# Ten gate and up chunks of the last FFN in pairs, by seven block products over both halves of the tokens

## The chip, the cores and the metric

One core of a Trainium2 chip. The metric is the device time of one execution in microseconds, as a median of runs. The engines are named as in the profile: PE (TensorE, matmuls), PEld (its weight loads), DVE (VectorE), ACT (ScalarE), POOL (GpSimd), SP (the engine that issues the DMAs).

## The reference

A trunk of two layers over 1024 tokens of 1024 channels, all in float32. Layer 0 mixes the tokens by two attention forms, layer 1 by a convolution module, and each layer ends with an FFN. What follows is what the change touches:

```python
def conformer_conv(h, ...):                 # layer 1
    a = h @ w_pw1 + b_pw1
    u = a[..., :D_MODEL] * jax.nn.sigmoid(a[..., D_MODEL:])
    u = lax.conv_general_dilated(u, w_dw, ...) + b_dw        # causal, 31 taps, each channel by itself
    u = (u - mu) * lax.rsqrt(var + EPS) * ln_g + ln_b        # over the channels
    return jax.nn.silu(u) @ w_pw2 + b_pw2

def swiglu(h, wg, wu, wd):                  # each layer; D_FF = 2816
    return (jax.nn.silu(h @ wg) * (h @ wu)) @ wd

for layer in range(2):
    h = h + mix(rms_norm(h, mix_norm[layer]))
    h = h + swiglu(rms_norm(h, ffn_norm[layer]), ffn_w_gate[layer], ffn_w_up[layer], ffn_w_down[layer])
```

## The kernel before

**Number format.** Every float32 operand is split into a high part and a low part, both of the type fp32r: ACT casts the high part, DVE subtracts it from the source (`split`, L95 to L101). A product is then three matmuls, high by high, high by low, low by high (`mm3`, L205 to L209).

**Tiling.** The tokens are worked on in two halves of 512, which is the moving side of a matmul: all matmuls here are of 128x512. The residual `xres` stands in SBUF as 8 tiles of 128 tokens. An FFN (`ffn_steps`) goes through its 2816 hidden channels in 22 chunks of 128; a chunk is a gate product and an up product, each of 8 K tiles by 3 matmuls, so 48 matmuls. Four chunks are collected, then two `down` steps, one for each half of the 1024 output columns, add act^T w into the residual, which DVE does from PSUM (L230). The weights of a chunk are loaded 256 columns at a time (1 MB) and split beside the matmuls.

**Layer 1.** The work is a list of steps that `run` traces in order; the weights of a step are traced one step ahead. In the names, f10 is the FFN of layer 1 for half 0 of the tokens and f11 that for half 1, p1 the first pointwise product of the convolution module for half 1, pw2 the second. A convolution (`conv_steps`) is 31 multiply-adds of DVE per 128 channels, 248 for a half, on `cv` tiles; `interleave` spreads them in pieces evenly behind the matmul steps given to it, and a piece may not begin before the DVE work of the step ahead of the last one. LayerNorm (`layer_norm`) transposes the `cv` tiles on PE into two PSUM buffers (tag "n", names plt), takes statistics and an inverse root on DVE (bst, mv, nv, nt, lrs, lnb), normalises on ACT (lx); the swish transposes back (pls), ACT makes ls and its high part sh, DVE the low part sl. LayerNorm of half 1 thus needs all 248 multiply-adds, and pw2 needs the swish.

The order of half 1's convolution module among the FFN of half 0 is this list (f10 has 34 steps: 22 chunks and 12 down steps):

```python
[lambda: add_bias(1), p1[0], norm_step(0, ffng[1], "f10")]
+ interleave(p1[1:] + f10[:21], conv_steps(1))
+ interleave(f10[21:27], ln1) + f10[27:-4] + pw2(1, s1) + [norm_step(1, ffng[1], "f11")]
+ f10[-4:] + [lambda: store(0, 0), lambda: store(0, 1)]
+ f11[:-1] + [lambda: store(1, 0), f11[-1], lambda: store(1, 1)]
```

**What sets the order.** When the program is built, a scheduler reorders the traced instructions and fixes one order for each engine; on the chip each engine runs its own list in that order and waits by semaphores. Tiles come from pools with a fixed number of buffers, so a load or a split also waits for the last reader of the buffer it takes. The pools `raw` (2 buffers of 8 KB a partition) and `ws` (8 of 4 KB) of the weights last for the whole program.

Of the kernel before, what the change touches and what calls it, by code (L numbers as in the profile page):

```python
# [18 lines left out]
P = 128  # L19
# [6 lines left out]
NF = DFF // P  # L26
EPS = 1e-6
# [7 lines left out]
def r32(ap):  # L35
    return ap.bitcast(F32)
# [3 lines left out]
def trunk(ctx, tc, x, mix_norm, ffn_norm, hy_w_in, hy_w_gate2, hy_b_gate, hy_gla_norm,  # L40
# [8 lines left out]
    raw_p = ctx.enter_context(tc.tile_pool(name="raw", bufs=2))  # L49
    ws_p = ctx.enter_context(tc.tile_pool(name="ws", bufs=8))  # L50
    dram = ctx.enter_context(tc.tile_pool(name="dram", bufs=1, space=DRAM))

# [7 lines left out]
    identr = const.tile([P, P], F32R, name="identr")  # L60
    nc.scalar.copy(identr, ident)
    maskr = const.tile([P, P], F32R, name="maskr")
    hones = const.tile([P, P], F32, name="hones")
    nc.vector.memset(hones, 0.0)
    nc.vector.memset(hones[0:64, 0:64], 1.0 / 64.0)
    nc.vector.memset(hones[64:128, 64:128], 1.0 / 64.0)

    # vectors, 128 channels to a row, transposed on chip into columns
# [34 lines left out]
    small = ctx.enter_context(tc.tile_pool(name="small", bufs=2))  # L103

    def inv_sqrt(y, ss, scale, name):
        """y = 1 / sqrt(ss * scale + eps), by Newton's iteration."""
# [12 lines left out]
    def x_tile(name, dt=F32):  # L119
        return hold.tile([P, 1056], dt, name=name, tag="x", bufs=8)  # L120
# [6 lines left out]
    def norm_stats(xt, junk, name):  # L127
        """1 / RMS of four token tiles."""
# [13 lines left out]
    def norm_half(xt, xn, rs, gcol, ps, pstag, name, muls):  # L142
        """Four token tiles scaled (into xn); returns the transposed hi and lo parts [D chunk, 8, 512]."""
# [11 lines left out]
    def load_cols(w, c0, name, n=256):  # L155
        """n columns of a weight with 1024 rows."""
        raw = raw_p.tile([P, NK, n], F32, name=f"raw_{name}", tag="raw")
        nc.sync.dma_start(raw, w[:, c0:c0 + n].rearrange("(k p) c -> p k c", p=P))
        return raw

    def load_rows(w, r0, n, j, name):
        """n chunks of 128 rows of a weight with 1024 columns, half j of the columns."""
# [10 lines left out]
    # A step is a function, or a pair (weights, body) whose weights are traced one such step ahead.  # L173
    def interleave(main, filler):
        """The main steps in order, with the filler steps spread evenly behind them."""
# [29 lines left out]
    def mm3(ps, sh, sl, mh, ml, first, last):  # L205
        """ps += s^T m by the three leading products of the hi and lo parts."""
        nc.tensor.matmul(ps, sh, mh, start=first, stop=False)  # L207
        nc.tensor.matmul(ps, sh, ml, start=False, stop=False)  # L208
        nc.tensor.matmul(ps, sl, mh, start=False, stop=last)  # L209

    def down(w, r0, acts, xt, tiles, ps, tag, j, name):
        """Step of x[tile] += act^T w over n K chunks, half j of the columns."""
# [25 lines left out]
    def ffn_steps(l, h, hT, xt, ps, ft, act, use_silu, group):  # L238
        raws, acts = {}, {}

        def weights(f):
            if f % 2 == 0:
                raws["g"] = load_cols(ffn_w_gate[l], P * f, f"g{l}{f}{h}")
                raws["u"] = load_cols(ffn_w_up[l], P * f, f"u{l}{f}{h}")
            return [parts(raws[t][:, :, P * (f % 2):P * (f % 2) + P], f"{t}{l}_{f}_{h}") for t in ("g", "u")]
# [21 lines left out]
        while f < NF:  # L267
            n = min(group, NF - f)
# [14 lines left out]
    # Activations that need a table stay between its load and the next one.  # L283
# [20 lines left out]
    # =====================================================================  # L304
    # layer 0: hybrid mixer
    # =====================================================================
# [706 lines left out]
```

## Time and profile before

| | us |
|---|---|
| median of 3 runs (lowest to highest) | 2323.39 (2320.95 to 2323.78) |
| span of the profiled execution | 2319.9 |
| PE busy, 10866 matmuls | 2290.3 (99%) |
| DVE busy | 1591.3 (69%) |
| ACT busy | 922.4 (40%) |
| convolution of half 1, first to last multiply-add | 1468.4 to 1782.2 |
| last matmul starts | 2315.93 |

The profile is of one execution; its busy time of an engine is the time in which at least one of its instructions ran. PE runs matmuls one into the other, so the mean duration of a matmul (391 ns) is longer than the distance between two of them. "Idle before" and the arrow behind it say how long an engine waited and what ended the wait.

### The profile page before, as it was taken

The numbers are of one execution on the slowest core, as the hardware profiler recorded it, in microseconds if no ns is written. First come the engines' busy times: TensorE is split into PE (matmuls) and PEld (weight loads), VectorE is DVE, ScalarE is ACT, GpSimd is POOL, SyncE is SP. The second block draws the span as 40 slices with busy tenths as digits, with TensorE's granted clock in tenths as the row PEclk, the third lists the DMA queues.
The fourth block names the chain that finished last, engine by engine and source line by source line (L and its number), as shares of the span: only waits on it lengthen the run. The fifth ranks groups of instructions, "written<-read, shape, count | busy, mean of one in ns | idle before, by whom it ended". The sixth has DMA issues, their size and how long they took to land.

```text
span 2319.9 us, 27940 instructions
## 1 busy us (share of the span) xinstructions
PE 2290.3 (99%) x10866; PEld 1899.1 (82%) x10866; DVE 1591.3 (69%) x2486; ACT 922.4 (40%) x1506; POOL 32.9 (1%) x39
## 2 busy tenths in 40 slices
PE   7999999999999999999999999999999999999999
PEld 6788888788888887788888888888888888888887
DVE  6687764877788656588888856789998545334334
ACT  6465545655565324523222245422222424222221
POOL 0000000000000001000000002000000000000000
PEclk9999999999999999999999999999999999999999
DMA  6254454233343235233222322322322223322322
GB/s 207 97 163 141 167 188 141 76 98 118 100 131 111 68 103 181 73 97 103 91 93 89 109 91 82 109 86 96 109 91 91 91 92 127 109 91 92 108 84 80
DMA packets 206387, 253.74 MB, mean 109 GB/s; under 512 B 8709, under 2 KB 156272, under 8 KB 206254
## 3 DMA queue, kind: packets, MB, share of 16 engines
q1 hardware_dynamic: 206254, 251.95, 33.5%
q8 instruction: 85, 1.39, 0.2%
q14 instruction: 48, 0.39, 0.1%
HBM read 230.95 MB, written 20.97 MB: 109 GB/s over the span
## 4 chain that ended last, share of the span: by engine, by line
PE 95%; DMA 2%; DVE 2%; ACT 1%; issue 0%; SPq 0%; ACTq 0%; DVEq 0%
PE po L207 9%; PE po L209 9%; PE po L208 9%; PE pu L207 7%; PE pu L209 7%; PE pu L208 7%; PE pg L207 7%; PE pg L209 7%; PE pg L208 7%; PE pp L208 2%; PE pp L207 2%; PE pp L209 2%; PE po L652 2%; PE wt L634 1%; PE z L617 1%; PE z L613 1%
## 5 line engine op out<-in xcount | busy, mean ns | idle before, releaser
L908 DVE SCALAR_TENSOR_TENSOR cv<-u,wd,cv 128x512 f32<-128x512 f32 x480 | 358.1, 749 | 9.9
L230 DVE TENSOR_TENSOR xr<-xr,po 128x512 f32<-128x512 f32 x296 | 202.1, 684 | 168.8 <-PE po L209 168.0
L207 PE MATMUL po<-wh_d,a 128*128 128x512 f32 x704 | 277.8, 395 | 1.7 <-DVE xr L230 1.6
L207 PE MATMUL pg<-hh_f,wh_g 128*128 128x512 f32 x704 | 275.8, 392 | 3.6 <-DVE s L260 3.6
L208 PE MATMUL pg<-hl_f,wh_g 128*128 128x512 f32 x704 | 276.6, 393 | 0.0
L209 PE MATMUL pg<-hh_f,wl_g 128*128 128x512 f32 x704 | 275.8, 392 | 0.0
L209 PE MATMUL po<-wh_d,a 128*128 128x512 f32 x704 | 275.5, 391 | 0.0
L208 PE MATMUL pu<-hl_f,wh_u 128*128 128x512 f32 x704 | 275.4, 391 | 0.0
L208 PE MATMUL po<-wl_d,a 128*128 128x512 f32 x704 | 275.2, 391 | 0.0
L209 PE MATMUL pu<-hh_f,wl_u 128*128 128x512 f32 x704 | 275.2, 391 | 0.0
L207 PE MATMUL pu<-hh_f,wh_u 128*128 128x512 f32 x704 | 275.0, 391 | 0.0
L97 ACT CAST wh_g<-raw_g 128x1024 fp32r<-128x1024 f32 x88 | 92.8, 1054 | 348.4 <-PE po L208 226.2
L97 ACT CAST wh_d<-raw_d 128x1024 fp32r<-128x1024 f32 x88 | 92.5, 1053 | 252.0 <-PE pu L208 116.7
L98 DVE TENSOR_TENSOR wl_g<-raw_g,wh_g 128x1024 fp32r<-128x1024 f32 x88 | 107.6, 1223 | 88.0 <-ACT wh_g L97 83.8
L207 PEld LDWEIGHTS po<-wh_d,a 128*128 128x128 f32 x704 | 132.3, 188 | 31.4 <-DVE xr L230 4.0
L207 PEld LDWEIGHTS pg<-hh_f,wh_g 128*128 128x128 f32 x704 | 132.6, 188 | 30.8 <-DVE s L260 3.8
L209 PEld LDWEIGHTS po<-wh_d,a 128*128 128x128 f32 x704 | 132.2, 188 | 27.8
L209 PEld LDWEIGHTS pg<-hh_f,wl_g 128*128 128x128 f32 x704 | 132.7, 189 | 27.0
L208 PEld LDWEIGHTS pu<-hl_f,wh_u 128*128 128x128 f32 x704 | 132.3, 188 | 27.3
L261 DVE TENSOR_TENSOR s<-s,pu 128x512 f32<-128x512 f32 x88 | 60.5, 687 | 137.1 <-PE pu L209 134.5
L208 PEld LDWEIGHTS pg<-hl_f,wh_g 128*128 128x128 f32 x704 | 132.6, 188 | 26.7
L209 PEld LDWEIGHTS pu<-hh_f,wl_u 128*128 128x128 f32 x704 | 132.2, 188 | 27.0
(318 smaller groups left out, 4300.3 us busy)
## 6 DMA issues: line engine op xcount, KB each, us to landing
raw_g<-in_ffn_w_gate_dram SPq DMA_DIRECT2D x44, 1024.0 KB
raw_u<-in_ffn_w_up_dram SPq DMA_DIRECT2D x44, 1024.0 KB
raw_d<-in_ffn_w_down_dram SPq DMA_DIRECT2D x30, 1024.0 KB
raw_p<-in_cv_w_pw_dram SPq DMA_DIRECT2D x16, 1024.0 KB
raw_d<-in_ffn_w_down_dram SPq DMA_DIRECT2D x28, 512.0 KB
raw_wo<-in_hy_w_out_dram SPq DMA_DIRECT2D x8, 1024.0 KB
raw_q<-in_cv_w_pw_dram SPq DMA_DIRECT2D x8, 1024.0 KB
kr<-k_d SPq DMA_DIRECT2D x48, 128.0 KB
```

The costliest lines, as they stand in the source:

```text
L97: nc.scalar.copy(hi, src)
L98: nc.vector.tensor_sub(lo, src, r32(hi))
L207: nc.tensor.matmul(ps, sh, mh, start=first, stop=False)
L208: nc.tensor.matmul(ps, sh, ml, start=False, stop=False)
L209: nc.tensor.matmul(ps, sl, mh, start=False, stop=last)
L230: nc.vector.tensor_add(xt[i][:, cs], xt[i][:, cs], po)
L261: nc.vector.tensor_mul(s, s, pr[1])
L613: nc.tensor.matmul(z, qs[:, sub(i)], kh[:, s0:s0 + w], start=True, stop=False)
L617: nc.tensor.matmul(z, qs[:, sub(i)], kl[:, s0:s0 + w], start=False, stop=True)
L634: nc.tensor.transpose(pt[:, col:col + P], wrow[bi][:, P * j:P * j + P], ident)
L652: nc.tensor.matmul(po[:, lo_c:256], st["v"][j // 4][:, j % 4, e, :], m[:, 256 * jj + lo_c:256 * jj + 256], start=(last and jj == 0 and m i ...
L908: i = nc.vector.scalar_tensor_tensor(acc, u[:, j:j + TH], wd[:, c, j:j + 1], acc, op0=ALU.mult, op1=ALU.add)
```

## The change

The number of FFN chunks that each half does by itself in layer 1 becomes `ALONE` = 12. The other ten are done in five pairs, for both halves of the tokens at once, after everything else. For a pair, the weight matrix is a block matrix of 2x2 (two blocks of 512 rows by two chunks), and so are the tokens (two blocks of 512 channels by two halves). Instead of the eight block products there are seven, of 4 K tiles by 3 matmuls each, on sums and differences of blocks (Strassen's algorithm in Winograd's form). The sums over the token blocks are made once (`sums`, `sum4`, on DVE and ACT, among the chunks of f11); those of the weights for each pair (`pair_weights`). Two of the seven products are evicted half way (to u by ACT, to v by DVE) and continued in the same PSUM tile by another product. The down steps of a pair then run over all eight token tiles.

Since f10 now has 18 steps, the list of half 1's convolution module changes: the convolution stands behind 7 + 10 steps instead of 7 + 21, LayerNorm behind 4 instead of 6, and no chunk stands between LayerNorm and pw2. The weight pools are closed after f10, and the rest runs with new pools that take the same room: smaller and more raw buffers, groups of 2 chunks, loads of 128 columns. All stores of the output are at the end. Constants of layer 0 are moved into its own pool.

```diff
+ALONE = 12
...
-    raw_p = ctx.enter_context(tc.tile_pool(name="raw", bufs=2))
-    ws_p = ctx.enter_context(tc.tile_pool(name="ws", bufs=8))
...
+    weights_es = ctx.enter_context(ExitStack())
+    raw_p = weights_es.enter_context(tc.tile_pool(name="raw", bufs=2))
+    ws_p = weights_es.enter_context(tc.tile_pool(name="ws", bufs=8))
...
-    def ffn_steps(l, h, hT, xt, ps, ft, act, use_silu, group):
+    def ffn_steps(l, h, hT, xt, ps, ft, act, use_silu, group, last=NF, wide=2):
...
-        f10 = ffn_steps(1, 0, lambda: hT["f10"], xres, ps, ft, act, True, 4)
-        f11 = ffn_steps(1, 1, lambda: hT["f11"], xres, ps, ft, act, True, 4)
+        f10 = ffn_steps(1, 0, lambda: hT["f10"], xres, ps, ft, act, True, 4, ALONE)
...
-               norm_step(0, ffng[1], "f10")] + interleave(p1[1:] + f10[:21], conv_steps(1))
-            + interleave(f10[21:27], ln1) + f10[27:-4] + pw2(1, s1) + [norm_step(1, ffng[1], "f11")]
-            + f10[-4:] + [lambda: store(0, 0), lambda: store(0, 1)]
-            + f11[:-1] + [lambda: store(1, 0), f11[-1], lambda: store(1, 1)])
+               norm_step(0, ffng[1], "f10")] + interleave(p1[1:] + f10[:-8], conv_steps(1))
+            + interleave(f10[-8:-4], ln1) + pw2(1, s1) + [norm_step(1, ffng[1], "f11")] + f10[-4:])
+    weights_es.close()
+    with ExitStack() as es:
+        raw_p = es.enter_context(tc.tile_pool(name="raw3", bufs=3))
+        ws_p = es.enter_context(tc.tile_pool(name="ws3", bufs=7))
...
+            BUFS = {"a": 6, "b": 2}
...
+        def product(pm, w, b, first=True, last=True):
+            for k in range(4):
+                mm3(pm, w[:, 0, k, :], w[:, 1, k, :], b[0][:, k, :], b[1][:, k, :], first and k == 0, k == 3,
+                    skip_group_check=not (first and last))
...
+        def pair_products(wt, nm, done):
+            pm = lambda i: ps.tile([P, 512], F32, name=f"ps{i}{nm}", tag="a")
+            p0 = pm(0)
+            product(p0, wt["11"], b11, last=False)
+            u = ft(f"u{nm}")
+            nc.scalar.copy(u, p0)
+            product(p0, wt["12"], b21, first=False)
+            done(0, 0, p0, None)
+            p1 = pm(1)
+            product(p1, wt["s2"], t2)
+            nc.vector.tensor_add(u, u, p1)
+            p2 = pm(2)
+            product(p2, wt["s3"], t3, last=False)
+            p3 = pm(3)
+            product(p3, wt["s1"], t1, last=False)
+            v = ft(f"v{nm}")
+            nc.vector.tensor_add(v, u, p3)
+            done(1, 1, p2, v)
+            product(p3, wt["s4"], b22, first=False)
+            done(0, 1, p3, u)
+            product(p2, wt["22"], t4, first=False)
+            done(1, 0, p2, u)
...
+        f11 = ffn_steps(1, 1, lambda: hT["f11"], xres, ps, s_tile, act, True, 2, ALONE, 1)
+        steps = interleave(f11, [lambda k=k: sums(k) for k in range(4)])
+        steps += [lambda k=k: sum4(k) for k in range(4)]
+        late = []
+        for f in range(ALONE, NF, 2):
+            mats, downs = pair_steps(1, f)
+            steps += mats[:1] + late + mats[1:]
+            late = downs
...
+        run(steps + [late[0], lambda: store(0), late[1], lambda: store(1)])
```

What this does to the built orders is shown at three places. In a row stand the line, the operation, what it writes and what it reads; numbers are part of the names.

PE before, at the last `cv` tile (cv17) of the convolution of half 1. plt10, plt11 are the transposes of the first and second token tile, pg1_16 and pg1_17 gate products of f10:

```order
L207 MATMUL pg1_16_0_14907<-hh_f10_12598,wh_g1_16_0_14757 128x512
L208 MATMUL pg1_16_0_14907<-hl_f10_12599,wh_g1_16_0_14757 128x512
L929 MATMUL plt101_14839<-ident_69,cv17_14589 128x128
L209 MATMUL pg1_16_0_14907<-hh_f10_12598,wl_g1_16_0_14758 128x512
...
L207 MATMUL pg1_17_0_15043<-hh_f10_12598,wh_g1_17_0_14899 128x512
L929 MATMUL plt110_14868<-ident_69,cv10_12723 128x128
...
L929 MATMUL plt110_14868<-ident_69,cv13_13537 128x128
L929 MATMUL plt111_14874<-ident_69,cv14_13769 128x128
...
L929 MATMUL plt111_14874<-ident_69,cv17_14589 128x128
L208 MATMUL pg1_17_0_15043<-hl_f10_12599,wh_g1_17_0_14899 128x512
```

PE after, at the same place, from the last matmul of a down product (po_3_1) on; pls10 are the first transposes of the swish:

```order
L204 MATMUL po_3_1_14472<-wh_d1_4_012_14333,a1_7_0_14011 128x512
L932 MATMUL plt101_14111<-ident_63,cv15_13601 128x128
L932 MATMUL plt101_14111<-ident_63,cv16_13765 128x128
L932 MATMUL plt101_14111<-ident_63,cv17_13929 128x128
L932 MATMUL plt110_14140<-ident_63,cv10_12723 128x128
...
L932 MATMUL plt110_14140<-ident_63,cv13_13209 128x128
L932 MATMUL plt111_14146<-ident_63,cv14_13437 128x128
...
L932 MATMUL plt111_14146<-ident_63,cv17_13929 128x128
L932 MATMUL plt120_14175<-ident_63,cv10_12723 128x128
...
L932 MATMUL plt131_14282<-ident_63,cv17_13929 128x128
L946 MATMUL pls10_14309<-ident_63,lx100_14093 128x128
```

The matmuls of f10 that stood between the transposes are gone from there; the transposes of all four token tiles follow each other.

DVE before, at the end of the convolution; wl are low parts of weights, s and a belong to FFN chunks, bst are the first statistics of LayerNorm:

```order
L908 SCALAR_TENSOR_TENSOR cv17_14589<-u71_13107,wd_8689,cv17_14589 128x512
L98 TENSOR_TENSOR a1_14_0_14735<-s1_14_0_14732,a1_14_0_14735 128x512
L908 SCALAR_TENSOR_TENSOR cv17_14589<-u71_13107,wd_8689,cv17_14589 128x512 x3
L98 TENSOR_TENSOR wl_g1_17_0_14900<-raw_g1160_14753,wh_g1_17_0_14899 128x1024
L908 SCALAR_TENSOR_TENSOR cv17_14589<-u71_13107,wd_8689,cv17_14589 128x512 x2
L261 TENSOR_TENSOR s1_15_0_14815<-s1_15_0_14815,pu1_15_0_14790 128x512
L98 TENSOR_TENSOR wl_u1_17_0_14904<-raw_u1160_14755,wh_u1_17_0_14903 128x1024
L98 TENSOR_TENSOR a1_15_0_14818<-s1_15_0_14815,a1_15_0_14818 128x512
L930 BN_STATS bst10_14829<-plt101_14839 128x6
```

DVE after, from its last add of a down product on (of the 32 convolution rows the first, some of the last and the final six, which are one row):

```order
L225 TENSOR_TENSOR xr3_3194<-xr3_3194,po_3_1_14472 128x512
L90 TENSOR_TENSOR wl_q0112_14520<-raw_q011_14513,wh_q0112_14519 128x1024
L911 SCALAR_TENSOR_TENSOR cv17_13929<-u71_13147,wd_8689,cv17_13929 128x512
L911 SCALAR_TENSOR_TENSOR cv16_13765<-u61_13064,wd_8689,cv16_13765 128x512
L911 SCALAR_TENSOR_TENSOR cv15_13601<-u51_12985,wd_8689,cv15_13601 128x512
...
L911 SCALAR_TENSOR_TENSOR cv17_13929<-u71_13147,wd_8689,cv17_13929 128x512
L911 SCALAR_TENSOR_TENSOR cv16_13765<-u61_13064,wd_8689,cv16_13765 128x512
L911 SCALAR_TENSOR_TENSOR cv17_13929<-u71_13147,wd_8689,cv17_13929 128x512 x6
L933 BN_STATS bst10_14101<-plt101_14111 128x6
L935 BN_AGGR mv10_14102<-bst10_14101 128x2
```

Between the last split and the statistics there are now 32 multiply-adds; before, the last ones stood among the splits and products of f10's chunks 14 to 17.

ACT before, at the first weights of f11; hh_f11 is the high part of the normalised tokens, pt_f11 their transposes, in brackets the semaphores that a row waits for:

```order
L97 CAST wh_d1_20_010_16064<-raw_d1_20_01_16062 128x1024 [waits DMAHW4_49,PE_49]
L100 ACTIVATE hh_f11_15876<-pt_f11_0_15878,vb_86 128x512 [waits PE_49]
L100 ACTIVATE hh_f11_15876<-pt_f11_1_15885,vb_86 128x512 [waits PE_49]
L97 CAST wh_g1_0_1_16104<-raw_g101_16100 128x1024 [waits DMAHW5_49,PE_49]
L100 ACTIVATE hh_f11_15876<-pt_f11_2_15892,vb_86 128x512 [waits PE_49]
L100 ACTIVATE hh_f11_15876<-pt_f11_3_15899,vb_86 128x512 [waits PE_49]
L97 CAST wh_u1_0_1_16108<-raw_u101_16102 128x1024 [waits DMAHW6_49,PE_49]
L100 ACTIVATE hh_f11_15876<-pt_f11_4_15906,vb_86 128x512 [waits PE_49]
```

ACT after, with the casts of the block sums (tt):

```order
L92 ACTIVATE hh_f11_14822<-pt_f11_7_14873,vb_73 128x512 [waits PE_49]
L89 CAST wh_g1_0_1_15171<-raw_g101_15167 128x1024 [waits DMAHW5_49,DVE_49,PE_49]
L89 CAST tt1_15165<-b22_0_15531 128x512 [waits DVE_49,Activation_49]
L89 CAST tt2_15166<-b12_0_15529 128x512
L89 CAST tt0_15164<-b11_0_15527 128x512
L89 CAST wh_u1_0_1_15175<-raw_u101_15169 128x1024 [waits DMAHW6_49]
L89 CAST wh_g1_1_1_15183<-raw_g111_15179 128x1024 [waits DMAHW7_49]
L89 CAST wh_u1_1_1_15187<-raw_u111_15181 128x1024 [waits DMAHW0_49]
L253 ACTIVATE s1_0_1_15241<-pg1_0_1_15191 128x512 [waits DVE_49,PE_49,Activation_49]
```

The cast of the first gate weights, which stood among the evictions of the norm, now stands behind them all, with the casts of the next weights in a row behind it.

## Rows read from the trace of the kernel before

**Rows 1.** The page: the span, then busy time, share and instructions of each engine.

```profile
span 2319.9 us, 27940 instructions
...
PE 2290.3 (99%) x10866; PEld 1899.1 (82%) x10866; DVE 1591.3 (69%) x2486; ACT 922.4 (40%) x1506; POOL 32.9 (1%) x39
```

**Rows 2.** Stretches: length, busy us (x) of PE, PEld, DVE, ACT, POOL; clock, DMA.

```profile
1468.40:1782.20 313.80, 313.80 (x1401) 259.79 (x1400) 285.97 (x376) 85.90 (x103) 1.09 (x5) 1.00 0.29 94
1782.20:1832.80 50.60, 50.60 (x242) 42.17 (x241) 33.18 (x90) 18.07 (x23) 0.00 (x0) 1.00 0.26 85
1960.00:2300.00 340.00, 340.00 (x1502) 281.62 (x1501) 130.28 (x146) 89.31 (x107) 0.00 (x0) 1.00 0.29 97
```

**Rows 3.** Timeline at the end: start us, us, engine, line, operation, count, idle before.

```profile
2315.25 0.39 PE L209 MATMUL po<-wh_d,a 128*128 128x512 f32 x1
...
2315.93 0.39 PE L209 MATMUL po<-wh_d,a 128*128 128x512 f32 x1
2316.36 0.69 DVE L230 TENSOR_TENSOR xr<-xr,po 128x512 f32<-128x512 f32 x1 [0.67 <-PE po L209]
```

**Rows 4.** Groups of DVE, 1468.4 to 1782.2: count, busy us, mean ns, idle before.

```profile
L908 DVE SCALAR_TENSOR_TENSOR cv<-u,wd,cv 128x512 f32<-128x512 f32 x240 | 178.2, 749 | 4.4
L98 DVE TENSOR_TENSOR wl_g<-raw_g,wh_g 128x1024 fp32r<-128x1024 f32 x18 | 22.0, 1223 | 3.7 <-ACT wh_g L97 3.3
...
L230 DVE TENSOR_TENSOR xr<-xr,po 128x512 f32<-128x512 f32 x24 | 16.4, 683 | 2.1 <-PE po L209 1.8
```

**Rows 5.** Timeline of DVE in the convolution of half 1.

```profile
1470.97 1.23 DVE L98 TENSOR_TENSOR wl_p<-raw_p,wh_p 128x1024 fp32r<-128x1024 f32 x1
1472.12 3.11 DVE L908 SCALAR_TENSOR_TENSOR cv<-u,wd,cv 128x512 f32<-128x512 f32 x4
...
1476.03 0.74 DVE L908 SCALAR_TENSOR_TENSOR cv<-u,wd,cv 128x512 f32<-128x512 f32 x1
...
1477.35 0.74 DVE L908 SCALAR_TENSOR_TENSOR cv<-u,wd,cv 128x512 f32<-128x512 f32 x1
```

**Rows 6.** Timeline of one token tile's LayerNorm, half 1: PE, DVE and ACT.

```profile
1809.24 1.04 PE L929 MATMUL plt<-ident,cv 128*128 128x128 f32 x8
...
1810.04 1.29 DVE L930 BATCH_NORM_STATS2 bst<-plt 128x6 f32<-128x512 f32 x2
...
1812.56 0.16 DVE L117 SCALAR_TENSOR_TENSOR lrs<-nt_l,lrs 128x1 f32<-128x1 f32 x1
...
1813.05 0.69 DVE L230 TENSOR_TENSOR xr<-xr,po 128x512 f32<-128x512 f32 x1 [0.33 <-PE po L209]
...
1813.65 0.15 DVE L115 TENSOR_TENSOR nt_l<-lrs 128x1 f32<-128x1 f32 x1
...
1814.81 0.16 DVE L934 SCALAR_TENSOR_TENSOR lnb<-mv,lrs 128x1 f32<-128x1 f32 x1
...
1815.09 1.45 ACT L936 ACTIVATE lx<-plt,lnb,lrs 128x512 f32<-128x512 f32 x2 [6.96 <-DVE lnb L934]
```

**Rows 7.** Timeline: transposes of the swish and the ACT work behind them.

```profile
1837.55 1.03 PE L943 MATMUL pls<-ident,lx 128*128 128x128 f32 x8
1838.19 1.45 ACT L945 ACTIVATE ls<-pls,vb 128x512 f32<-128x512 f32 x2 [0.74 <-PE pls L943]
```

**Rows 8.** Timeline of PE around its longest wait, and a stretch as in rows 2.

```profile
455.94 0.50 PE L207 MATMUL pg<-hh_f,wh_g 128*128 128x512 f32 x1 [3.62 <-DVE s L260]
...
457.43 0.62 PE L207 MATMUL pg<-hh_f,wh_g 128*128 128x512 f32 x1
457.85 0.63 PE L208 MATMUL pg<-hl_f,wh_g 128*128 128x512 f32 x1
...
458.00:459.00 1.00, 1.00 (x4) 0.80 (x3) 0.75 (x2) 0.42 (x1) 0.00 (x0) 0.50 0.06 16
459.00:460.00 1.00, 1.00 (x4) 0.71 (x4) 0.69 (x1) 0.20 (x1) 0.00 (x0) 0.50 0.00 0
```

**Rows 9.** Groups of ACT, 1960 to 2300: count, busy us, mean ns, idle before.

```profile
L97 ACT CAST wh_g<-raw_g 128x1024 fp32r<-128x1024 f32 x20 | 21.0, 1052 | 98.4 <-PE po L208 67.2 <-PE pg L208 28.5 <-DMA raw_g<-in_ffn_w_gate_dram 2.7
```

More of the change, by code (lines that the diff above doesn't have):

```diff
@@ L59, in trunk @@
     nc.vector.memset(one_t, 1.0)
[L60 to L66, printed above, removed]
     rows = lambda ap: ap.rearrange("(k p) -> k p", p=P)
@@ L119, in x_tile @@
     def x_tile(name, dt=F32):
-        return hold.tile([P, 1056], dt, name=name, tag="x", bufs=8)
+        return hold.tile([P, D], dt, name=name, tag="x", bufs=8)
     def h_tile(name):
@@ L203, in run, with mm3 @@
                 s()
[L205 to L209, printed above, removed]
+    def mm3(ps, sh, sl, mh, ml, first, last, **kw):
+        nc.tensor.matmul(ps, sh, mh, start=first, stop=False, **kw)
+        nc.tensor.matmul(ps, sh, ml, start=False, stop=False, **kw)
+        nc.tensor.matmul(ps, sl, mh, start=False, stop=last, **kw)
     def down(w, r0, acts, xt, tiles, ps, tag, j, name):
@@ L235, in sub @@
         return slice(P * (i % 4), P * (i % 4) + P)
-    def ffn_steps(l, h, hT, xt, ps, ft, act, use_silu, group):
+    def ffn_steps(l, h, hT, xt, ps, ft, act, use_silu, group, last=NF, wide=2):
         raws, acts = {}, {}
         def weights(f):
[L242 to L245, printed above, removed]
+            if f % wide == 0:
+                raws["g"] = load_cols(ffn_w_gate[l], P * f, f"g{l}{f}{h}", P * wide)
+                raws["u"] = load_cols(ffn_w_up[l], P * f, f"u{l}{f}{h}", P * wide)
+            c0 = P * (f % wide)
+            return [parts(raws[t][:, :, c0:c0 + P], f"{t}{l}_{f}_{h}") for t in ("g", "u")]
         def chunk(f, ws):
@@ L266, in ffn_steps @@
         steps, late, f = [], [], 0
-        while f < NF:
-            n = min(group, NF - f)
+        while f < last:
+            n = min(group, last - f)
             for c in range(f, f + n):
@@ L362, in trunk @@
         t_tile = lambda name, dt=F32: tp.tile([P, 512], dt, name=name, tag="t")
+        identr = gp.tile([P, P], F32R, name="identr")
+        nc.scalar.copy(identr, ident)
+        maskr = gp.tile([P, P], F32R, name="maskr")
+        hones = gp.tile([P, P], F32, name="hones")
+        nc.vector.memset(hones, 0.0)
+        nc.vector.memset(hones[0:64, 0:64], 1.0 / 64.0)
+        nc.vector.memset(hones[64:128, 64:128], 1.0 / 64.0)
         mtmp = ft("mtmp")
@@ L968, in norm_step @@
             return lambda: hT.update({name: norm(h, gcol, name)})
-        def store(h, j):
-            for i in range(4 * h, 4 * h + 4):
-                cs = slice(512 * j, 512 * j + 512)
-                nc.sync.dma_start(xout[i * P:(i + 1) * P, cs], xres[i][:, cs])
         p0 = pw1_steps(0, lambda: hT["c0"])
```

84 lines of the change are left out of this document (added).

## The prediction

> **What bounds the kernel now.** I read the totals first, then stretches by engine, then single rows. TensorE is busy 99% of a 2319.9 us span, with VectorE at 69% [rows 1]. In the three stretches of layer 1 that the change touches, PE is busy in every microsecond, at full granted clock, while DVE uses 286.0 of 313.8 us, 33.2 of 50.6 and 130.3 of 340 [rows 2]. So until now a matmul taken out of this part is time taken out, and a wait put in is time put in; but in the first stretch DVE has only 9% to spare, and it is the causal convolution that fills it. That is the place to watch.
>
> The profiled execution has a span of 2319.9 us and the median of the runs is 2323.39, 3.5 us above it. I make the sum on the span and add 3.5.
>
> **Matmuls removed.** A 128x512 matmul starts 0.2267 us after the one before: (2315.93 − 2315.25)/3 [rows 3]. The built orders hold 10824 PE instructions before and 10704 after. Ten chunks lose 2 matrices x 2 halves x 24 = 960 matmuls and get 5 pairs x 2 matrices x 7 products x 12 = 840. 120 x 0.2267 = **−27.2 us**, if PE stays fed. No other part of the edit can gain, since PE has no idle time there to give back.
>
> **The convolution loses its cover.** Its DVE instructions for half 1 of the tokens were spread over 28 steps of matmul work and are now spread over 17, because the first half's FFN of layer 1 ends at chunk 12. The built orders give, from the end of the first pointwise chunk to the last transposes of the convolution's result, 1406 matmuls before and 1008 after: about 321 us of PE work against 231 (transposes included). What DVE does between its first and last convolution instruction falls only by 15 weight splits (1.22 us each) and 18 adds or products of 512 columns (0.68 each) [rows 4], 30 us, and by some 10 more since more convolution instructions alternate between two results (below): from 286 to about 245.5. DVE now has more work than PE.
>
> Where this ends is seen in the order. DVE's last add on a down product, xr3 from po_3_1, belongs to the last matmul before the transposes. Behind it DVE has one weight split and 32 convolution instructions, and PE has nothing but transposes that need the last of them. Convolution instructions that alternate with another result start every 0.66 us ((1477.35 − 1476.03)/2); in a chain on one result they start every 0.78 (four in 3.11); a weight split takes 1.15 to the next start (1472.12 − 1470.97) [rows 5]. 27 x 0.666 + 5 x 0.78 = 21.9; with the split (1.15) and the add (0.61) 23.7. PE waits at least about that; the start of the add, 0.43 us behind the start of the last matmul (2316.36 − 2315.93 [rows 3]), and the way back add some 0.8. I take **+24.5 us**. The lower end is 23.6; the upper is DVE idling 9% of the stretch as it did before: 245.6/0.911 − 231.3 = 38.
>
> **LayerNorm loses its cover too.** Before, 139 matmuls stood between the transposes of the first and of the last token tile, and 110 more among the swish; now 0 and 36. The chain of a tile was hidden; now it is the path. The two PSUM buffers of a tile come free only when ACT has normalised it, so the next tile's second transposes wait for that. From the rows of one tile: the second statistics instruction starts about 0.61 behind the first, 1810.65, and the last small DVE step at 1814.81; an unrelated add costs 0.9 of that (from 1812.56 + 0.19 to 1813.65), so 3.26. ACT starts 0.28 later and takes 1.45 for both halves [rows 6]. Four transposes and the hand-off to the next engine are 0.64 (1837.55 to 1838.19) [rows 7]. One tile: 0.64 + 3.26 + 0.28 + 1.45 = 5.6. First tile to its ACT 3.8, three periods 16.9, half a normalisation 0.8: 21.5, of which 25 transposes at 0.1 us are work: **+19 us** (17 to 24).
>
> The swish then starts with little ready: the first pw2 product needs transposes, swish (0.73) and cast, about 2 us, beside 12 transposes that PE can do: **+1.5** (1 to 4).
>
> **The clock.** Before, PE waited 3.62 us once, for DVE; its next matmuls ran at full pace for 1.5 us, and then 8 of them started 0.42 apart instead of 0.23, at a granted clock of 0.50, the lower level of 1.2 GHz, in the stretch 458 to 460 [rows 8]: 8 x 0.2 = 1.6 us, for a single wait. The change has about 45 us of waiting with only transposes in between, in two or three pieces. I take **+3** (1.6 to 10; the upper end is all transposes and the 36 matmuls of the swish at half clock).
>
> The Trainium skill, "TensorE: Matmul & The Clock Gate", section "HAM oscillation — how this bites in real kernels", says that waits which recur between bursts of matmuls let the array fall back to its lower clock each time, so that every burst starts slow. The row above agrees with it for one wait. By the rule at its worst, every burst of the LayerNorm and swish at the lower level, the sum is 7 us higher.
>
> **The new pools.** The first weights of half 1 no longer share pools with the work before: the new pools lie over the old ones, so the cast of the first gate weights waits on ACT for the last matmul of half 0, where it used to stand among the norm's evictions. ACT's cast takes 1.05 [rows 9], then come a few matmuls, then the lower part's split (1.22 [rows 4]). Behind that cast on ACT stand casts for the block sums and the next weights. About 2.1; I take **+2.5** (1.5 to 5, if the next chunk's loads, which wait for the same, come late).
>
> **Inside the seven products.** Two products per matrix are evicted in the middle (to ACT by a copy, to DVE by an add) and then go on in the same PSUM tile. In PE's order at least 12 matmuls, 2.7 us, of other products stand between, but for one place. An ACT step of 1024 columns is 1.05, a DVE step of 512 is 0.68, so this is covered; and DVE's work per pair, by my count 36 us of instructions at rows 4's durations, fits beside 264 matmuls, 59.8 us. **+1.5** (0 to 10). Loads are issued 11 to 50 us of matmul work ahead, and DMA moved 97 GB/s on average in such a stretch [rows 2] with room. The stores of all eight tiles now come at the end, but the last add stays where it was: 0.
>
> **Sum.** −27.2 + 24.5 + 19 + 1.5 + 3 + 2.5 + 1.5 = +24.8. Span 2344.7, time **2348** us, 1.1% slower. Lower ends: −27.2 + 23.6 + 17 + 1 + 1.6 + 1.5 = +17.5, time 2341. With the convolution at its upper end: 2362.
>
> **Rivals.**
> A, faster: DVE and PE overlap where I let them follow one another. If only DVE's load counts, the convolution costs 245.5 − 231.3 = 14.2; and if the statistics of the next tile run while ACT normalises the last, a tile adds only 0.64 + 0.28 + 1.45 = 2.4, 7 for three. −27.2 + 14.2 + 7 + 1.5 = −4.5: 2319. It decides where both waits together stay below 27 us. For it speaks that DVE never ran behind PE in the old stretch [rows 2]; against it the order, in which 32 convolution instructions stand between the last add and the first statistics, and rows 6, where ACT waits for the last small step. 5%.
>
> B, no change: the convolution's wait comes as computed, but LayerNorm hides most of its own, 4 us left: −27.2 + 23.6 + 4 = 0, 2323. It needs matmuls between the tiles, and the order has none. 4%.
>
> C, the products are not covered: each matrix's two mid-way evictions expose 1 us, a wait such as the add's 0.43 plus 0.6 to its end [rows 3], 10 x 2 x 1 = 20 us instead of 1.5: 2367. For it: PSUM tiles are held longer than in any row of before. Against: the 12 matmuls between. 8%.
>
> D, the clock stays low through the whole LayerNorm and swish, +7: 2355. [rows 8] show it for one wait. 8%.
>
> That the change does not do what it says is excluded for the matmuls by the count of 120 in the built order.
>
> **How the numbers follow.** Forecast 75%, A 5, B 4, C 8, D 8. The likeliest is 2348. From 2340 to 2366 lie the forecast with the bounds of its terms and D, and the edge of C; A and B are left out, and part of C. A measurement of this kernel tells about 0.2%, 4.6 us, from no change: faster is A, 0.05; same is B, 0.04; slower the rest, 0.91.
>
> **What the new profile should show.** PE idle of 23 to 26 us in one piece ahead of the last transposes of the convolution's result, released by DVE's convolution line, with the 32 instructions before it on DVE. Four periods of 5 to 6 us in which PE does only transposes, released by ACT's normalisation. A granted clock below 1.00 in the slices behind them. One idle of 1 to 3 us at the first gate matmul of half 1's FFN. In the stage of the pairs a PE that is busy nearly throughout, and 120 fewer matmuls. I am wrong if the wait before LayerNorm is under 15 us, if matmuls stand between the tiles' transposes, or if the pairs show waits at each mid-way eviction.

## The result, and the profile after

The changed kernel takes **2350.1 us** (median; 2346.99 to 2350.54) against 2322.97 for the kernel before in the same comparison: a ratio of 1.0115, 95% interval 1.0100 to 1.0129. It is slower, by 27 us; 2348 was forecast.

The top of its page, to be held against [rows 1]: 120 matmuls fewer, PE busy 97% instead of 99%, and one slice of forty in which the granted clock fell to half.

```profile
span 2345.2 us, 27972 instructions
...
PE 2270.6 (97%) x10746; PEld 1881.2 (80%) x10746; DVE 1689.9 (72%) x2704; ACT 929.5 (40%) x1552; POOL 32.8 (1%) x39
...
PEclk9999999999999999999999999999959999999999
```

Where the time is lost stands in the chain of work that ended last, here from the convolution's tail to the swish (start, us, engine, what, line, count):

```profile
1696.29 17.90 DVE cv L911 x27
1714.22 0.76 DVE cv L911
...
1718.69 0.71 DVE bst L933
1722.17 0.79 ACT lx L939
1723.00 1.98 PE plt L932 x8
1725.01 0.71 DVE bst L933
1728.55 0.79 ACT lx L939
1729.38 1.98 PE plt L932 x8
...
1738.56 0.59 DVE b L1019
...
1742.79 1.13 PE pls L946 x4
```

The first rows are the convolution that nothing covers: 27 multiply-adds in 17.90 us and five more at some 0.78, of which one is shown: exactly the 32 of the order. From 1696.29 to the first transpose behind them at 1718.17 it is 21.9 us, and the sum by [rows 5] was 21.9. Then the chain goes round once for each token tile: statistics on DVE, normalisation on ACT, transposes on PE, statistics again. In the last tile an add for the block sums of the pairs (b) has come between, 0.59 us. PE's own waits from here to the end add it up (what PE waited to do, for whom: us in total, times, longest):

```profile
PE plt L932 <- DVE cv L911: 24.1, 3, 11.2
PE plt L932 <- ACT lx L939: 13.3, 3, 4.5
PE pls L946 <- ACT lx L939: 5.0, 1, 5.0
PE po L202 <- DVE xr L225: 1.6, 3, 0.9
PE pg L202 <- ACT wh_g L89: 1.1, 1, 1.1
PE pg L204 <- DVE wl_g L90: 0.5, 1, 0.5
```

24.1 us for the convolution; 13.3 and 5.0 for LayerNorm; the 5.0 has the add for the block sums in it, and is 4.5 in the runs below where no such add stands there. The next three are the first products of half 1's FFN and a few down products. There is no wait at all on the copies u and v of the seven products.

The clock in these stretches (columns as in [rows 2]): 0.50 through LayerNorm, where the eight transposes of a tile take 1.98 instead of 1.04 [rows 6]; and once more, at 1843, in the first products of half 1's FFN.

```profile
1692.90:1718.17 25.27, 1.18 (x4) 0.36 (x2) 25.04 (x36) 1.04 (x1) 0.00 (x0) 0.57 0.13 41
1718.17:1742.79 24.62, 6.38 (x25) 4.88 (x25) 14.58 (x68) 5.17 (x8) 0.00 (x0) 0.50 0.00 0
1742.79:1748.00 5.21, 5.13 (x19) 4.22 (x20) 1.37 (x3) 4.39 (x7) 0.00 (x0) 0.54 0.00 0
...
1843.00:1846.00 3.00, 3.00 (x9) 2.30 (x8) 3.00 (x5) 1.35 (x2) 0.00 (x0) 0.53 0.61 174
```

Two executions differ in their early part too. The same small copy of half 1's convolution, which has the same PE instructions ahead of it in both programs, stands at 1441.94 before,

```profile
1441.94 0.21 POOL L878 COPY u<-halo 128x30 f32<-128x30 f32 x1 [13.87 <-PE pt_c L151]
```

and 3.5 us earlier after:

```profile
1438.45 0.21 POOL L881 COPY u<-halo 128x30 f32<-128x30 f32 x1 [13.89 <-PE pt_c L146]
```

In the profiles of the experiments this copy stands anywhere from 1439.6 to 1442.9 us, so where two profiles are set against each other below, the time is taken from this copy to the end. It is 877.96 us before and 906.75 after: 28.8 us are to be explained, and the parts are: −27.2 for 120 matmuls; +24.1 and +18.3 of waits; +6.5 of half clock in LayerNorm and at the swish (the figure of the first experiment); +1.7 of waits and 1.5 of half clock at the first products of half 1's FFN; +1.6 at down products. That is 26.5. The other 2.3 us were not assigned row by row; the first matmul behind a wait, 0.33 instead of 0.23 us to the next, is part of them.

### The profile page after: what moved, and what is told of

It is laid out like the page before. It is cut to its first block, busy times and chain, and to the rows that moved or that the text cites. A ratio compares the mean times of both kernels' runs of the same rounds, so it can differ in the third digit from the quotient of the medians.

```text
span 2345.2 us, 27972 instructions
## 1 busy us (share of the span) xinstructions
PE 2270.6 (97%) x10746; PEld 1881.2 (80%) x10746; DVE 1689.9 (72%) x2704; ACT 929.5 (40%) x1552; POOL 32.8 (1%) x39
## 4 chain that ended last, share of the span: by engine, by line
PE 92%; DVE 3%; ACT 2%; DMA 2%; issue 1%; SPq 0%; ACTq 0%; DVEq 0%
PE po L202 9%; PE po L203 9%; PE po L204 9%; PE pu L202 5%; PE pu L204 5%; PE pu L203 5%; PE pg L204 5%; PE pg L202 5%; PE pg L203 5%; PE pp L203 2%; PE pp L202 2%; PE pp L204 2%; PE po L655 2%; PE wt L637 1%; DVE cv L911 1%; PE z L620 1%
## 5 line engine op out<-in xcount | busy, mean ns | idle before, releaser
L202 PE MATMUL pg<-hh_f,wh_g 128*128 128x512 f32 x544 | 214.4, 394 | 4.7 <-DVE s L256 3.6
L202 PE MATMUL po<-wh_d,a 128*128 128x512 f32 x544 | 214.7, 395 | 3.1 <-DVE xr L225 2.9
L203 PE MATMUL pg<-hl_f,wh_g 128*128 128x512 f32 x544 | 214.5, 394 | 0.0
L204 PE MATMUL pg<-hh_f,wl_g 128*128 128x512 f32 x544 | 213.9, 393 | 0.5 <-DVE wl_g L90 0.5
L203 PE MATMUL pu<-hl_f,wh_u 128*128 128x512 f32 x544 | 213.1, 392 | 0.0
L204 PE MATMUL pu<-hh_f,wl_u 128*128 128x512 f32 x544 | 212.9, 391 | 0.0
L202 PE MATMUL pu<-hh_f,wh_u 128*128 128x512 f32 x544 | 212.7, 391 | 0.0
L203 PE MATMUL po<-wl_d,a 128*128 128x512 f32 x544 | 212.3, 390 | 0.0
L204 PE MATMUL po<-wh_d,a 128*128 128x512 f32 x544 | 212.1, 390 | 0.0
L202 PEld LDWEIGHTS pu<-hh_f,wh_u 128*128 128x128 f32 x544 | 102.2, 188 | 20.4
L203 PEld LDWEIGHTS po<-wl_d,a 128*128 128x128 f32 x544 | 102.3, 188 | 20.0
```

Source lines behind the costliest of these rows:

```text
L202: nc.tensor.matmul(ps, sh, mh, start=first, stop=False, **kw)
L203: nc.tensor.matmul(ps, sh, ml, start=False, stop=False, **kw)
L204: nc.tensor.matmul(ps, sl, mh, start=False, stop=last, **kw)
```

## The experiments

The theory: the seven products save what they should, and the loss is the cover that the convolution and LayerNorm of half 1 had from ten chunks of half 0's FFN. The main rival: the pairs' own stage or its new pools hold part of the loss. All ratios are to the kernel before, with 95% intervals.

### The order alone

In the kernel before, only the list is changed:

```diff
-  interleave(p1[1:] + f10[:21], conv_steps(1)) + interleave(f10[21:27], ln1) + f10[27:-4] + pw2(1, s1)
-  + [norm_step(1, ffng[1], "f11")] + f10[-4:] + ...
+  interleave(p1[1:] + f10[:10], conv_steps(1)) + interleave(f10[10:14], ln1) + pw2(1, s1)
+  + [norm_step(1, ffng[1], "f11")] + f10[14:] + ...
```

> The kernel before, no pairs, no new pools: only the list is changed, so that the convolution of half 1 has the same 17 steps beside it as in the changed kernel, LayerNorm the same 4, and the other chunks of half 0's FFN come behind pw2. The built order around the convolution and LayerNorm is that of the changed kernel, row for row. Theory (lost cover): the waits of the changed kernel come back in full, 24.1 us for the convolution, 18.3 in LayerNorm and about 6.6 of half clock: 2323 + 49 = 2372 us (2366 to 2376). Rival (the stage of the pairs or the new pools hold a good part of the loss): less, 2335 to 2360.

Measured: 2370.4 us, 1.0203 (1.0189 to 1.0217). PE's waits in it:

```profile
PE plt L929 <- DVE cv L908: 24.1, 3, 11.2
PE plt L929 <- ACT lx L936: 13.3, 3, 4.5
...
PE pls L943 <- ACT lx L936: 4.5, 1, 4.5
```

They are those of the changed kernel to a tenth of a microsecond but for the last, and no pair, no new pool and no sum is in this program. The page gives PE's busy time for the same 10866 matmuls as before:

```profile
PE 2296.8 (97%) x10866; PEld 1903.6 (80%) x10866; DVE 1581.1 (67%) x2486; ACT 923.1 (39%) x1506; POOL 32.9 (1%) x39
```

It is 6.5 us above [rows 1]: the price of the half clock in and behind LayerNorm, with the slower first matmul behind each wait in it. 24.1 + 13.3 + 4.5 + 6.5 = 48.4; from the copy to the end this run is 48.1 us longer than before, and its median is 47 above. The changed kernel loses 54 us in all, the 27 that were measured and the 27.2 that the products should save. So the order alone costs 47 of the 54. The rival keeps the other 7, which the next run and the one on the pools divide.

### The seven products alone

The changed kernel with the eight plain products in each pair: four PSUM tiles of two products, no block sums.

```diff
-            p0 = pm(0)
-            product(p0, wt["11"], b11, last=False)
-            ...
+            for i, j in ((0, 0), (1, 1), (0, 1), (1, 0)):
+                p = pm(2 * i + j)
+                product(p, wt[f"{i + 1}1"], (b11, t4)[j], last=False)
+                product(p, wt[f"{i + 1}2"], (b21, b22)[j], first=False)
+                done(i, j, p, None)
```

> The changed kernel with all its staging and pools, but each pair by its eight plain block products: four PSUM tiles of two products each, no sums of token or weight blocks, nothing evicted half way. 120 matmuls more. Theory: the seven products give their whole 27.2 us, since nothing in their stage is exposed but the 1.6 us of waits that the trace shows: 2350 + 27 = 2377 us (2373 to 2380). Rival (hand-offs and sums of the seven products take back part of what they save): 2352 to 2370.

Measured: 2373.0 us, 1.0215 (1.0201 to 1.0229), 22.9 above the changed kernel where 27 were expected, at the lower edge of what the theory gave (from the copy to the end the two profiles differ by 22.6). So some 4 us of the 27.2 do not arrive, and the profiles tell where they stay. In this run PE waits 1.9 us instead of 3.3 behind the start of the swish, and 4.5 instead of 5.0 ahead of it, as no block sum stands in DVE's chain. At the first products of half 1 the clock stays at 1.00, where the changed kernel loses 1.5 us; the run on the pools tells why this part can't be put down to the products. About 1 us is left open.

### Four taps less

The changed kernel, half 1 of the convolution with 27 taps of 31:

```diff
-  piece(c, 8 * q, min(8 * q + 8, TAPS))
+  piece(c, 8 * q, min(8 * q + 8, TAPS - 4 * h))
```

> The changed kernel with the last 4 of 31 taps of the convolution left out for half 1 of the tokens (32 instructions of DVE); this part of the result is not computed. In the built order 4 multiply-adds stand behind the last split instead of 32. Theory: the wait ahead of LayerNorm falls from 24.1 to 3 to 6 us, LayerNorm's own 18.3 and its half clock stay: 2350 - 20 = 2330 us (2326 to 2334). Rival (the transposes wait for something else, such as PSUM buffers, and the wait only changes its name): above 2340.

Measured: 2330.2 us, 1.0031 (1.0019 to 1.0043). PE's waits:

```profile
PE plt L932 <- ACT lx L939: 13.3, 3, 4.5
...
PE plt L932 <- DVE cv L911: 6.1, 1, 6.1
PE pls L946 <- ACT lx L939: 5.0, 1, 5.0
```

18 us of the wait for the convolution are gone and LayerNorm's are the same to the tenth. So that wait was for DVE's multiply-adds, and the rival is out. The 6.1 us that are left lie just above the 3 to 6 that were expected.

### A shorter chain in LayerNorm

One Newton step instead of three for the inverse roots of half 1:

```diff
-        for _ in range(3):
+        for _ in range(1 if name.startswith("l1") else 3):
```

> The changed kernel with one Newton step instead of three for the inverse roots of half 1's LayerNorm (less exact there): six small DVE instructions of 0.195 us less in each token tile's chain; the order is otherwise the same. Theory (LayerNorm's chain through DVE is the path, tile after tile): four times 1.17 us less waiting: 2350 - 4.7 = 2345.5 us, PE's waits for ACT's normalisation 18.3 - 4.7 = 13.6. Rival (its tiles wait for ACT or PSUM, DVE has slack): unchanged, 2349 to 2351.

Measured: 2344.7 us, 1.0096 (1.0079 to 1.0113); by the profile:

```profile
PE plt L932 <- ACT lx L939: 9.8, 3, 3.3
...
PE pls L946 <- ACT lx L939: 3.8, 1, 3.8
```

9.8 + 3.8 = 13.6 instead of 18.3, as worked out from six small instructions of 0.195 us in each of four tiles. Instructions of one element a partition, hidden until now, have become path.

### The pools

The same new pools, with those of the weights opened behind four others, so that they lie over tiles of the convolution:

```diff
-        raw_p = es.enter_context(tc.tile_pool(name="raw3", bufs=3))
-        ws_p = es.enter_context(tc.tile_pool(name="ws3", bufs=7))
         tp3 = ...   # t3, act3, ft3, s3
+        ws_p = es.enter_context(tc.tile_pool(name="ws3", bufs=7))
+        raw_p = es.enter_context(tc.tile_pool(name="raw3", bufs=3))
```

> The changed kernel with the new pools opened in another order, so that the weights of half 1's FFN lie over room that is free long before (tiles of the convolution) and not over the last weights of half 0. In the built order the first gate cast then waits for its load alone. Theory: the wait of 1.1 + 0.5 us at the first gate matmul of half 1, the eight matmuls at half clock behind it (1.7) and the restarts go: 2350 - 4 = 2346 us, the granted clock there 1.00. Rival (the weights come late for another reason, such as DMA): unchanged.

What it removes, in the changed kernel:

```profile
1839.85 1.04 ACT L89 CAST wh_g<-raw_g 128x1024 fp32r<-128x1024 f32 x1 [12.78 <-PE po L204]
...
1840.95 0.50 PE L202 MATMUL pg<-hh_f,wh_g 128*128 128x512 f32 x1 [1.14 <-ACT wh_g L89]
...
1842.21 0.50 PE L204 MATMUL pg<-hh_f,wl_g 128*128 128x512 f32 x1 [0.53 <-DVE wl_g L90]
...
1843.30 0.63 PE L202 MATMUL pg<-hh_f,wh_g 128*128 128x512 f32 x1
...
1843.73 0.63 PE L203 MATMUL pg<-hl_f,wh_g 128*128 128x512 f32 x1
```

The cast starts when the last matmul of half 0 ends, the first product waits 1.14 us for it and the third 0.53 for the low part; then, at 1843.3, after 1 us of matmuls at full pace, products start 0.43 us apart. With the pools moved, measured: 2346.1 us, 1.0100 (1.0085 to 1.0115), and the granted clock in the same place:

```profile
1842.00:1844.00 2.00, 2.00 (x9) 1.65 (x10) 2.00 (x4) 0.00 (x0) 0.00 (x0) 1.00 0.04 8
1844.00:1846.00 2.00, 2.00 (x10) 1.64 (x10) 1.93 (x4) 1.09 (x2) 0.00 (x0) 1.00 0.00 0
```

0.87 us of waiting is left (for a down product's add), and the clock does not fall. The median is 4 us lower, as expected, but its interval overlaps that of the changed kernel; the profile bears it out with 4.1 us from the copy to the end. Of these 0.8 are waits at the first products, 0.5 is the block sum, which now stands elsewhere in DVE's order, and some 1.5 are the clock; the rest is in small pieces.

That the clock stayed up because of the move is not shown. The same two waits of 1.13 or 1.14 and 0.53 us stand in six of the other runs, with the clock at half behind them in three (four taps less, one Newton step, two banks) and at 1.00 in three (the fill, the cover given back, three pairs). In the last of these, the 3 us behind the second wait:

```profile
1882.90:1885.90 3.00, 2.97 (x13) 2.48 (x14) 3.00 (x6) 2.18 (x3) 0.00 (x0) 1.00 0.58 164
```

### Matmuls for nobody in the waits

Two runs, since the fill needs a PSUM bank: first the changed kernel with two buffers instead of three for down products,

```diff
-            BUFS = {"a": 3, "b": 3, "n": 2}
+            BUFS = {"a": 3, "b": 2, "n": 2}
```

> The changed kernel with two PSUM buffers instead of three for down products in layer 1. This is the ground for the next run, which needs the eighth bank. The built order has 23 multiply-adds behind the last split instead of 32 and the same empty LayerNorm. Both theories: about as the changed kernel, 2346 to 2356 us.

then the same with the free bank written by matmuls in each wait of LayerNorm:

```diff
+                    pd = ps.tile([P, 512], F32, name=f"pfill{i}", tag="d")
+                    for q in range(18 if i else 12):
+                        nc.tensor.matmul(pd, hT["f10"][0][:, 0, 0:P], hT["f10"][0][:, 1, :], ...)
```

> As the run with two banks, and in each of the four waits of half 1's LayerNorm matmuls of 128x512 whose result nobody reads, in the free bank: 12 in the first wait, 18 in each of the next. They add 66 matmuls and no work that is needed. Theory (the transposes there take 0.24 us instead of 0.1 because the clock is down): clock back to 1.00 from the second tile on, transposes of 24 + 12 at full pace and no slow first products: 5 us less than the run with two banks (3 to 7). Rival (transposes are slow for another reason, the fill only adds): 0 to 5 us more.

Measured: 2348.6 us with two banks, 1.0109 (1.0094 to 1.0124), and 2344.7 with the fill, 1.0092 (1.0077 to 1.0107): 3.9 less with 66 matmuls more. The intervals overlap; from the copy to the end the fill is 4.9 us shorter, as expected, but 1.5 of that lie at the first products of half 1, where the clock stayed up this time. The clock in LayerNorm is plain. Two of LayerNorm's periods with two banks,

```profile
1724.00:1730.00 6.00, 1.97 (x8) 1.57 (x8) 3.69 (x17) 1.08 (x2) 0.00 (x0) 0.50 0.00 0
1730.00:1736.00 6.00, 1.97 (x8) 1.57 (x8) 3.69 (x17) 1.01 (x2) 0.00 (x0) 0.50 0.00 0
```

and the first three with the fill:

```profile
1720.00:1726.00 6.00, 5.81 (x18) 4.58 (x19) 3.13 (x17) 1.45 (x2) 0.00 (x0) 0.54 0.00 0
1726.00:1731.00 5.00, 4.71 (x24) 3.62 (x22) 3.60 (x17) 0.67 (x1) 0.00 (x0) 1.00 0.00 0
1731.00:1737.00 6.00, 5.42 (x26) 4.11 (x27) 3.67 (x17) 1.61 (x4) 0.00 (x0) 1.00 0.00 0
```

The first twelve matmuls run at the lower level of 1.2 GHz (0.54), behind 20 us in which PE did three transposes; from then on it is 1.00 to the end of the swish, where it was 0.50 without them.

### The cover given back

For each pair, the even chunk of half 0 needs nothing of half 1. It is done as a plain chunk of f10, with its down product; its first product is kept in DRAM for the pair, which does the other five:

```diff
+        f10 = ffn_steps(1, 0, ..., 4, ALONE, 2, [[12, 14, 16], [18, 20]], keep)   # 12 chunks and 5 even ones
+  interleave(p1[1:] + f10[:15], conv_steps(1)) + interleave(f10[15:21], ln1) + pw2(1, s1)
+  + [norm_step(1, ffng[1], "f11")] + f10[21:]
...
+                    if f >= last and k == 3:      # in chunk(): half of the K tiles are in
+                        keep(t, f, pm)            # ACT copies PSUM, a DMA stores it
...
-            product(p0, wt["11"], b11, last=False)
-            product(p0, wt["12"], b21, first=False)
+            u = wt["u"]                           # loaded again
```

> The changed kernel, with work moved ahead that needs half 0 alone: of each pair, the two products for its even chunk and half 0 are done as a plain chunk of half 0's FFN, with its down product; the first product is stored to DRAM when half done and loaded again for the other five. As many matmuls as the changed kernel, but 17 chunks beside the convolution and LayerNorm instead of 12. In the built order 6 multiply-adds close the convolution with matmuls beside them, and 64, 33 and 0 matmuls stand between the token tiles of LayerNorm. Theory: the convolution's wait is 0 to 2, LayerNorm keeps one period (4.5) and the start of the swish (5) and some half clock (2): 2323 - 27.2 + 3 + 12 = 2311 us (2304 to 2316). Rival (DRAM round trip, or norm of half 1 left with too little beside it): 2320 or more.

Measured: 2320.4 us, 0.9983 (0.9974 to 0.9991): 30 us better than the changed kernel with the same number of matmuls, but 9 worse than expected: outside the range of the theory and in that of the rival (the eleven runs took 2315.7 to 2321.6). The convolution's wait is gone, as 327 us of PE without a gap show, and what is left of LayerNorm's is in 20 us (columns as in [rows 2]):

```profile
1443.00:1770.00 327.00, 327.00 (x1468) 270.22 (x1466) 291.67 (x430) 103.61 (x136) 2.39 (x7) 1.00 0.31 100
1770.00:1790.00 20.00, 10.98 (x50) 8.79 (x49) 10.03 (x38) 9.05 (x15) 0.00 (x0) 0.66 0.08 32
```

Those 9 us of waits were foreseen, in sum. Where the rest lies is told by the distances from one start on PE to the next, as far as they are above the usual 0.2267 us, or 0.10 for a transpose. LayerNorm and the swish lose 13.8 us in all, where 11.5 had been put (4.5, 5 and 2). Around the first products of half 1 it is 3.0, of which 1.6 are waits there. The stage of the pairs loses 7.9, where that of the changed kernel loses 2.8, nearly all of it at down products: with one chunk for half 0 a PSUM tile takes three matmuls, 0.68 us, as long as DVE's add into the residual [rows 4], and PE waits for that add. (PE's waits for it, 4.8 us over the program against 3.5, show only part of this.) That had not been foreseen. Together it is 24.7, where 15 had been put.

### All of it covered

The last run with the pools moved, three PSUM buffers for those down products, and two of the moved chunks tied to their place: each of their gate and up products, 24 matmuls or 5.4 us, must stand between two tiles' transposes.

```diff
+                        if h == 1 and (i, j, k) == (3, 0, 0):
+                            behind(tr, ends["1_16_0"][7][1])      # 4th tile behind a gate product
...
+                    behind(ends["1_16_0"][0][0], trs[2])          # which stands behind the 3rd
+                    behind(ends["1_16_0"][8][0], trs[3])
...
-            BUFS = {"a": 6, "b": 2}
+            BUFS = {"a": 5, "b": 3}
```

> The run with the cover back, with three more edits: two of the moved chunks are held by order so that 60, 24, 24 and 24 matmuls stand ahead of the second, third and fourth token tile and of the swish; the new pools lie over room that is free early; down products of the pairs have three PSUM buffers instead of two. As many matmuls as the changed kernel. Theory: 27.2 saved, no wait in LayerNorm, none at the first gate matmul, 2 to 3 us at the swish and 3 at the down products: 2323 - 27.2 + 8 = 2304 us (2299 to 2310). Rival (moving work ahead costs DVE or DMA time elsewhere): 2312 or more.

Measured: **2308.4 us**, 0.9937 (0.9924 to 0.9949), faster than both kernels. The page, and the stretches up to LayerNorm, LayerNorm with the swish, and the rest:

```profile
span 2307.0 us, 28086 instructions
...
PE 2265.9 (98%) x10746; PEld 1876.6 (81%) x10746; DVE 1702.9 (74%) x2716; ACT 930.3 (40%) x1548; POOL 32.8 (1%) x39
```

```profile
1443.00:1753.00 310.00, 310.00 (x1388) 256.37 (x1387) 281.17 (x405) 96.48 (x126) 1.30 (x6) 1.00 0.31 100
1753.00:1790.00 37.00, 31.52 (x156) 24.68 (x155) 22.95 (x66) 19.46 (x29) 0.00 (x0) 1.00 0.46 150
1790.00:2300.00 510.00, 504.71 (x2239) 416.07 (x2239) 337.22 (x493) 153.28 (x227) 0.00 (x0) 1.00 0.28 87
```

The clock is 1.00 throughout, and 5.5 us of waits stand in LayerNorm and the swish, where the convolution's tail, LayerNorm and the swish lost 49 in the changed kernel. The other waits are 5.3 us. So about half of the 27.2 us arrives. Of the 10.8 us of waits 2.1 are for the copies of the products that are kept for the pairs, 2.4 for the casts of a pair's activations ahead of its down products, and 1.7 for the eviction to v half way in the seven products. No other run waits for that one; this run has five PSUM buffers for the products instead of six, but that they are the cause is not shown.

### Three pairs instead of five

```diff
-ALONE = 12
+ALONE = 16
```

> The changed kernel with the one number ALONE = 16 instead of 12: three pairs instead of five, so 72 matmuls saved instead of 120, and four more chunks in half 0's FFN. In the built order matmuls stand beside the end of the convolution again, but 34, 0 and 0 between the token tiles of LayerNorm. Theory: -16.3 for the products, 9 + 5 for two tiles and the swish, 5 at half clock, 6 at the new pools and down products: 2323 + 9 = 2332 us (2325 to 2337). Rival (four chunks more cover all of it): 2311.

Measured: 2330.8 us, 1.0032 (1.0019 to 1.0044). Four chunks more cover the convolution, for which PE no longer waits, but the scheduler set most of their matmuls ahead of LayerNorm. The token tiles and the swish still wait 15.8 us: cover must stand in the right place, not only be there.

## Why the prediction was right

- **Matmuls removed, −27.2.** 120 fewer on the page; the products give it, as the run with eight products shows within the 4 us named there, which are waits and clock as far as they are assigned.
- **The convolution, +24.5.** 24.1. The tail read from the order, 32 multiply-adds behind the last matmul's add, is the chain's rows one for one.
- **LayerNorm, +19.** 18.3 of waits, tile by tile 4.4 to 5.0. A tile's period was 6.4, where 5.6 was worked out: longer by the half clock of the transposes, which stands below. 0.5 of the 18.3 is the add for the block sums in the last tile, which the term did not have.
- **The swish, +1.5.** Nothing: the first products stand right behind their transposes, which took 3.2 us at half clock. In the run with the fill, at full clock, PE waits 0.3 us there.
- **The clock, +3.** Mis-sized: 6.5 in LayerNorm and at the swish, midway between the term and the 10 us of the rival that had the clock low through all of both. The term was taken from a single wait [rows 8] (the longest behind the first 14 us of the program, in which there are two longer ones). But the 24 transposes of three token tiles, the first 12 of the swish and the first four products behind them ran at half clock. The rival was right in LayerNorm; at the swish it was too high, as most of its products had the full clock. The Trainium skill, "TensorE: Matmul & The Clock Gate", section "HAM oscillation — how this bites in real kernels", is borne out by the trace in that every burst of transposes between two waits ran slow, at 0.50.
- **The new pools, +2.5.** 1.7 of waits, and 1.5 of half clock that the term did not have, and that came in some runs and not in others.
- **Inside the seven products, +1.5.** 1.6, but not where it was put: at down products, and none at the copies half way. The rival of exposed hand-offs (20 us) is out for this kernel.
- **Faster, or the same,** fall with the two waits: neither tile nor convolution overlapped more than the order let them.

The sum was 24.8; the span rose by 25.3 and the median by 27. Part of this agreement is luck: the swish's 1.5 too much stand against 5 us of clock too little, and the early part of this execution was 3.5 us shorter than that of before, which no term had. From the copy to the end, the part that the terms are about, it is 28.8, so the sum was 4 us short.

## What to carry to other kernels

Work that is taken out of one stage may have been the cover of another. Before matmuls are removed, list what runs beside them on the other engines, and count in the new order what stands between the last matmul's consumer and the next matmul that needs a long chain; those instructions times their durations are the wait. If the saving can be had by moving work as well as by removing it, move what depends least to where the chain is bare, and tie it there, since a scheduler that sees it ready sets it too early.

## What the runs showed of the hardware

- **Two short waits can cost as much again in clock, and need not.** At the first products of half 1, two waits of 1.14 and 0.53 us within 2.5 us were followed, 1 us later, by 3 us at a granted clock of 0.53, 1.5 us lost. With the same waits it was so in four runs of seven; in the other three the clock stayed at 1.00, as it did behind a wait of 0.87 in the run with the pools moved, and behind 1.13 and 0.21 in the run with eight products. What decides it is open.
- **Bursts of transposes between waits did not bring the clock back.** In the changed kernel three bursts of eight in 20 us stayed at 0.50; with matmuls of 128x512 in the waits the transposes had 1.00 from the second token tile on.
- **Splits on VectorE and adds on GpSimd held each other up.** In the changed kernel GpSimd adds four tiles of 128x1024, the first two in 2.40 us each, the others in 3.38 and 3.40:

```profile
1413.10 11.46 POOL L966 TENSOR_TENSOR xr<-xr,bb 128x1024 f32<-128x1024 f32 x4 [25.17 <-ACT xn_c L141]
```

In that time two weight splits of DVE, which read two tiles in SBUF, take 5.44 us, and a single one behind it 1.21. An add of DVE that reads a PSUM tile took 0.69 meanwhile, as elsewhere [rows 4].

```profile
1416.84 5.44 DVE L90 TENSOR_TENSOR wl_q<-raw_q,wh_q 128x1024 fp32r<-128x1024 f32 x2
...
1424.71 1.21 DVE L90 TENSOR_TENSOR wl_q<-raw_q,wh_q 128x1024 fp32r<-128x1024 f32 x1
```

Their ends fit turns, each instruction at its usual 2.4 or 1.2 us as soon as the other engine's has ended, but no run tests that. For this reason the low parts of the weights were not moved to the idle GpSimd, the next idea to free DVE beside the convolution.
